# One encoder layer on one core: forward segments, maxima, unread products and the split of a matrix in other places of the program

## The chip, the cores and the metric

The kernel runs on one core of one Trainium2 chip. The engines work side by side, each through its own queue of instructions in order: TensorE (PE, with its weight loads PEld), VectorE (DVE), ScalarE (ACT), GpSimd (POOL) and SyncE (SP, which issues most DMA transfers). The metric is the device time of one execution in microseconds (us), lower is better.

## What is computed

One layer over 2048 tokens of width 1024: a normed input projected into all branches, a gated linear recurrence in both directions (4 heads, chunks of 64), dense attention (8 heads), a gated merge, a mixture of 64 experts of which each token takes two, and a gated projection of per-layer inputs. Cut to what matters here:

```python
h = rmsnorm(x, ln_mix); z = h @ w_in
# recurrence, in both directions, per head:
#   S_t = diag(f_t) S_{t-1} + k_t v_t^T ;  o_t = S_t^T q_t ; then a norm of o per head and a gate
# attention, per head and block of queries:
s = einsum('bhqd,bhkd->bhqk', q, k) * scale
o = einsum('bhqk,bhkd->bhqd', softmax(s), v)
x += w_out(sigmoid(g_A) * w_oA(A) + sigmoid(g_B) * w_oB(B))
# experts: top-1 group, top-2 in it
x += sum over two experts of weight * (silu(h @ w1[e]) * (h @ w3[e])) @ w2[e]     # h = rmsnorm(x)
x += (p @ w_ple_proj) * sigmoid(rmsnorm(x) @ w_ple_gate)
```

## The kernel before

All large products are made of three products of fp32r halves (`mm3`, lines 96 to 101): each operand is split into a high part, a copy by ACT, and a low part, a subtraction by DVE or POOL. The stages follow one another, and in each the order of every engine's instructions is the order in which the Python code emits them (`manual_schedule`). Side work is written as generators that are advanced by `next` at fixed places, so that their instructions fall between those of the main lane.

*Start* (`stage_in`, line 175). The first token tile's rows are loaded, squared, scaled and turned by eight TensorE transposes (L199) before the first product; until then TensorE has nothing to do.

*Recurrence* (`hgrn`, line 884). 16 segments (4 heads, 4 segments each, from the last token back), eight steps each. In a step the main lane does one level of `hgrn_levels`; `gates` is advanced twice, which gives nine gate products of 128x512 (L860); and `side` advances the lanes that follow a segment: `hgrn_tail`, which makes the backward outputs and saves what the forward direction needs, and, once a head's last segment is through, `hgrn_forward`, which goes over that head's four segments from the front. One forward segment is a chain that is cut by `yield`: DVE updates the state four times (h_sf, L758), PE multiplies it with the queries into h_pf (L764), DVE adds the backward outputs (L766), ACT squares (L771), DVE makes the norm (L773 to L776, ten small operations and four larger ones, h_so), PE transposes h_so into h_pf (L781), and ACT copies the result out as h_a (L784). h_pf has one buffer. `hgrn_forward` (L790) starts a segment every three of its steps, and advances all lanes in each step, the oldest first.

*Attention* (`attention`, line 964). A softmax needs the row maxima of the scores before the scores are made, so each block of 512 queries has eight `max_step`s (L1005): two 96x512 products into t_pm, which has one buffer, and a DVE reduction of them (L1015). For the first block these are made at the start, with gate products between them (`run(n)` advances `gates`, two for a chunk of nine); K and V come by SP's queue. Then the main loop makes, for each of 16 key tiles of a block (kt), the scores of a later tile (three products, t_ps), the low part of its exponentials, the products with V (two), and at every second kt one max step of the next block (`maxima`), ahead of the scores. At kt 11 alone it stands at the end of the step; the maxima of the block before it are written in that step (`rows1`).

*Merge and routing* (`merge_out`, line 1627). Per token tile: products, residual, norm, transposes (`turn`), logits, and a chain of small operations on DVE (`route`), which needs TensorE at two places (`products`, at RANKS and SLOTS). The routes of the last tile end the stage; the experts' rows are then gathered by POOL through an index table.

*Experts* (`experts`, line 1947). 64 experts, in six positions each; a product of position i uses weights that were split three positions ahead on ACT (L1984) and DVE (L1986). In nine of them (`PROJ`, every fourth from 29 on) two products of w_ple_proj with p stand beside. Its weights are loaded at expert 28 and split at the last position of the same expert (L2094, L2095).

*Last stage* (`ple`, line 2186): the rest of these projections (`project`), the experts' sums (`add`), the norm, and the gate's products.

## Time and profile before

| | |
|---|---|
| time, median of 3 runs | 3376.83 us (3375.84 to 3383.98) |
| profiled execution | 3377.6 us, of which the span of instructions 3375.8 |
| busy share | PE 96%, PEld 80%, DVE 74%, ACT 60%, POOL 35% |
| instructions | 50147 |
| mean granted clock of TensorE | 0.987 |
| DMA | 599.81 MB, mean 178 GB/s |

A profile has for each engine the time in which it is busy, and rows of single instructions with their start and duration; a bracket behind a row gives the idle time of that engine just before, and what ended it. Matmul rows overlap, since the engine is pipelined: what a product costs is the distance from its start to that of the next. The granted clock (1.00 or 0.50 in most stretches) is the share of TensorE's full 2.4 GHz that the chip gave. Products of the same shape take twice as long at half.

### The profile page before, as it was taken

To read this page: it belongs to the slowest core of one execution; us is meant where nothing else is said; L and a number is where in the kernel's file an instruction comes from. 1 tells how busy PE (TensorE), PEld (TensorE's weight loads), DVE (VectorE), ACT (ScalarE), POOL (GpSimd) and SP (SyncE) were. 2 spreads that over 40 slices of the span, in tenths; PEclk is the share of its full clock that TensorE was granted. 3 is DMA by queue.
4 is the path that set the end of the run, shared out by engine and by line. 5 is a ranking of instruction groups with operands and counts; after the bars stand their busy time and mean duration, and the time that the engine had idled before them with its cause. 6 is when DMAs were issued, how large, how long until landed. Compare 5 with 4: busy or idle time off the path is not lost. (4 is left out here: it accounts for less than half of the span.)

```text
span 3375.8 us, 50147 instructions
## 1 busy us (share of the span) xinstructions
PE 3251.5 (96%) x17616; PEld 2690.4 (80%) x17616; DVE 2490.3 (74%) x4364; ACT 2020.8 (60%) x3610; POOL 1181.8 (35%) x869
## 2 busy tenths in 40 slices
PE   7999999999989999999999999999979999999899
PEld 7898989777767787777777777878868878888687
DVE  5666555467788747888888885645679989999775
ACT  5454544457666636888888884212248888888522
POOL 0000000144445426888888883000012222222243
PEclk9999999999999999999999999999989999999999
DMA  5756574633354252111111105866469899999542
GB/s 171 246 180 210 172 230 149 240 126 107 104 184 150 82 152 78 49 46 49 46 49 27 43 17 171 239 211 227 152 238 373 323 332 354 377 364 353 200 172 112
DMA packets 340607, 599.81 MB, mean 178 GB/s; under 512 B 59168, under 2 KB 209984, under 8 KB 328063
## 3 DMA queue, kind: packets, MB, share of 16 engines
q1 hardware_dynamic: 319246, 551.55, 48.9%
q0 software_dynamic: 20688, 43.45, 3.6%
q8 instruction: 140, 2.29, 0.3%
q10 hardware_dynamic: 416, 1.57, 0.1%
q14 instruction: 117, 0.95, 0.1%
HBM read 470.47 MB, written 159.51 MB: 187 GB/s over the span
## 5 line engine op out<-in xcount | busy, mean ns | idle before, releaser
L1048 POOL TENSOR_TENSOR t_za<-t_za,t_ph 128x512 f32<-128x512 f32 x384 | 498.0, 1297 | 66.1 <-ACT t_ph L1040 45.5
L1986 DVE TENSOR_TENSOR e_wl<-e_raw,e_wh 128x1024 fp32r<-128x1024 f32 x384 | 459.4, 1220 | 48.6 <-ACT e_wh L1984 40.4
L1984 ACT ACTIVATE e_wh<-e_raw 128x1024 fp32r<-128x1024 f32 x384 | 403.0, 1069 | 26.4 <-DMA e_raw<-in_w_dram 24.0
L1015 DVE TENSOR_REDUCE t_mx<-t_pm 128x1 f32<-128x1024 f32 x256 | 313.3, 1224 | 99.4 <-PE t_pm L1014 96.5
L1040 ACT ACTIVATE t_ph<-t_ps 128x512 fp32r<-128x512 f32 x512 | 305.2, 596 | 121.7 <-PE t_ps L1038 102.3
L1053 DVE TENSOR_TENSOR t_pl<-t_ps,t_ph 128x512 fp32r<-128x512 f32 x512 | 343.0, 683 | 32.1 <-ACT t_ps L1041 27.2
L860 PE MATMUL g_pm<-g_h,g_wh 128*128 128x512 f32 x1024 | 337.5, 411 | 4.6 <-DMA g_h<-d_ht 2.7
L1041 ACT ACTIVATE t_ps<-t_ps 128x512 f32<-128x512 f32 x512 | 303.7, 593 | 0.0
L2038 POOL DMA_INDIRECT d_y<-e_raw,sly x64 | 71.8, 1121 | 469.4 <-ACT e_raw L2036 439.2
L860 PEld LDWEIGHTS g_pm<-g_h,g_wh 128*128 128x128 f32 x1024 | 184.0, 190 | 47.9 <-DMA g_h<-d_ht 3.4
L663 POOL TENSOR_TENSOR h_qq<-h_qq,h_ff 128x512 f32<-128x512 f32 x112 | 169.1, 1515 | 149.8 <-DVE h_ff L666 87.4
L99 PE MATMUL e_pg<-e_wh,e_xh 128*128 128x512 f32 x512 | 207.5, 405 | 1.6 <-ACT e_wh L1984 1.2
L100 PE MATMUL e_pg<-e_wl,e_xh 128*128 128x512 f32 x512 | 203.6, 398 | 3.4 <-DVE e_wl L1986 3.3
L1036 PE MATMUL t_ps<-t_ql,t_kh 96*128 96x512 f32 x512 | 204.9, 400 | 0.1
L101 PE MATMUL e_pg<-e_wh,e_xl 128*128 128x512 f32 x512 | 204.3, 399 | 0.6 <-DVE e_xl L1973 0.6
L1065 PE MATMUL t_pa<-t_ph,vt 128*128 128x512 f32 x512 | 203.9, 398 | 0.0
L860 PE MATMUL g_pm<-g_h,g_wl 128*128 128x512 f32 x512 | 202.8, 396 | 0.5 <-DVE g_wl L836 0.5
L1066 PE MATMUL t_pb<-t_pl,vt 128*128 128x512 f32 x512 | 202.3, 395 | 0.1
L1037 PE MATMUL t_ps<-t_qh,t_kl 96*128 96x512 f32 x512 | 202.3, 395 | 0.0
L1038 PE MATMUL t_ps<-t_qh,t_kh 97*128 97x512 f32 x512 | 202.2, 395 | 0.0
L99 PE MATMUL pm<-whi,hh 128*128 128x288 f32 x640 | 194.2, 304 | 8.1 <-ACT csb L352 4.0
L100 PE MATMUL pm<-wlo,hh 128*128 128x288 f32 x640 | 190.4, 298 | 1.0 <-DVE nx_v L215 1.0
(447 smaller groups left out, 8640.4 us busy)
## 6 DMA issues: line engine op xcount, KB each, us to landing
e_raw<-in_w_dram SPq DMA_DIRECT2D x256, 512.0 KB
e_raw<-in_w_dram SPq DMA_DIRECT2D x64, 1024.0 KB
wraw<-in_w_in_dram SPq DMA_DIRECT2D x48, 512.0 KB
wraw<-in_w_in_dram SPq DMA_DIRECT2D x40, 576.0 KB
g_wr<-in_w_in_dram SPq DMA_DIRECT2D x38, 512.0 KB
d_g<-g_o SPq DMA_DIRECT2D x64, 256.0 KB
m_g<-d_g SPq DMA_DIRECT2D x64, 256.0 KB
p_y<-d_y SPq DMA_DIRECT2D x16, 1024.0 KB
```

The costliest lines, as they stand in the source:

```text
L99: nc.tensor.matmul(out, ah, bh, start=start, stop=False)
L100: nc.tensor.matmul(out, ah, bl, start=False, stop=False)
L101: nc.tensor.matmul(out, al, bh, start=False, stop=stop)
L860: nc.tensor.matmul(pm, p, q, start=k == 0 and i == 0, stop=k == KC - 1 and i == 2)
L1015: nc.vector.tensor_reduce(mx[n, i][:, j:j + 1], pm.rearrange("p a b -> p (a b)"), axis=AX, op=OP.max)
L1036: nc.tensor.matmul(ps, kh[0:QK, ks], ql[0:QK], start=True, stop=False)
L1040: nc.scalar.activation(ph, ps, AF.Exp)
L1041: nc.scalar.activation(ps, ps, AF.Exp)
L1048: nc.gpsimd.tensor_tensor(za[n], za[n], ph.bitcast(F32), op=OP.add)
L1053: nc.vector.tensor_tensor(pl, p, ph.bitcast(F32), op=OP.subtract)
L1984: nc.scalar.activation(hi, raw, AF.Copy)
L1986: nc.vector.tensor_tensor(lo, raw, hi.bitcast(F32), op=OP.subtract)
```

## The change

Seven edits, in the order of the program. (1) At the start, POOL clears a row of hl, and 24 products of it with itself go to a buffer that nobody reads. (2) A forward segment starts every four steps; one more `yield` stands before its transposes. (3) In attention's beginning, `gates` is advanced six times before the max steps, not twenty, and twice behind each of the three `maxima` that precede the loop, not once; V's split follows the third max step. (4) In attention's loop the last two max steps of a block (kt 13 and 15) are emitted behind the scores. (5) In the merge's tail unread products of the identity stand at four places, and 20 before expert 0's transposes. (6) `PROJ` starts at expert 30; the load of w_ple_proj stays at expert 28, and its split goes to the end of expert 29. (7) In the last stage the parts of the next projection are made before the first `yield` of `project`, and `add(1)` stands ahead of the loop.

```diff
@@ -317,6 +317,11 @@
         gB = const.tile([128, D], F32, name="gB")
         nc.scalar.dma_start(gB, bcast_rows(ln_mix[0], D))
         hh, hl, xt, v = open_norm(0, 1)
+
+        nc.gpsimd.memset(hl[:, 0].bitcast(F32), 0.0)
+        pm = psum.tile([128, 512], F32, name="pm", bufs=2)
+        for _ in range(24):
+            nc.tensor.matmul(pm, hl[:, 0, 0:128], hl[:, 0], start=True, stop=True)
         raws = load_raw(*todo[0][1:3])
         xt += [load_x(i) for i in range(1, 4)]
         squares(hh, xt[0], v, 0)
@@ -776,6 +781,7 @@
             nc.vector.scalar_tensor_tensor(so[:, c], op[:, c], r[:, c:c + 1], so[:, c], op0=OP.mult, op1=OP.mult)
         yield
         yield
+        yield
         pt = psum.tile(SH, F32, name="h_pf", bufs=1)
         for c in range(HC):
             nc.tensor.transpose(pt[:, c], so[:, c], g.ident)
@@ -787,7 +793,7 @@
     lanes = []
     for seg in range(NTB):
         lanes.append(segment(seg))
-        for _ in range(3):
+        for _ in range(4):
             for lane in lanes:
                 next(lane, None)
             yield
@@ -1144,11 +1150,11 @@
         for tb in range(NTB):
             load_k(h, tb)
         vr = load_v(h)
-        for _ in range(NTB):
-            run(5)
-        split_v(h, vr)
+        run(6)
         for s in range(8):
             max_step(0, s)
+            if s == 2:
+                split_v(h, vr)
             if s == 4 and NB > 1:
                 load_q(1)
             run(2)
@@ -1157,7 +1163,7 @@
         rows1(0)
         for u in range(-MAX_LEAD, 0):
             maxima(u)
-            run(1)
+            run(2)
         late.work, late.psum = more()
         for u in range(LEAD):
             scores(u)
@@ -1186,10 +1192,12 @@
             if kt == 14:
                 sums1(n)
 
-            if kt != 16 - MAX_LEAD:
+            if kt < 16 - MAX_LEAD:
                 maxima(u)
             if u + LEAD < NB * NK:
                 scores(u + LEAD)
+            if kt > 16 - MAX_LEAD:
+                maxima(u)
             if u + LEAD - 1 < NB * NK:
                 low(u + LEAD - 1)
             if kt == 1:
@@ -1734,6 +1742,12 @@
             step(r)
             if r.state is not END:
                 return
+
+    def idle(n):
+
+        py = psum.tile([128, 512], F32, name="m_py", bufs=OUT_BANKS["m_py"])
+        for _ in range(n):
+            nc.tensor.matmul(py[:, 0:128], g.ident, g.ident, start=True, stop=True)
 
     def advance(n, weave=()):
 
@@ -1777,12 +1791,16 @@
     advance(0, norm(NU - 1))
     after(PRE_B)
     products()
+    idle(8)
     turn(NU - 1)
     turned(NU - 1)
+    idle(2)
     logits(NU - 1)
     advance(100)
+    idle(6)
     products()
     logged(NU - 1)
+    idle(14)
     while routes:
         for r in list(routes):
             if r.state not in (RANKS, SLOTS):
@@ -1917,7 +1935,7 @@
 PRE, PRE_A, PRE_B = 8, 4, 2
 PRES = ((2, 48), (2, 60), (2, 72), (2, 84))
 MORE_LAST = 48
-PROJ = range(29, 29 + 4 * 9, 4)
+PROJ = range(30, 30 + 4 * 9, 4)
 
 
 def stage_moe(tc, g, w1, w3, w2, p, w_proj, ln_ple, out):
@@ -2042,6 +2060,10 @@
     proj, units = None, iter(range(T // 128))
     for i in range(3):
         split(i)
+
+    pt = psum.tile([128, 4, 128], F32, name="e_pt")
+    for _ in range(20):
+        nc.tensor.matmul(pt[:, 0], g.ident, g.ident, start=True, stop=True)
     for h in range(2):
         turn(0, h)
         turned(0, h)
@@ -2049,7 +2071,7 @@
         with_proj = e in PROJ
         if e and e + NX - 1 < NE:
             moe_gather(nc, g, xgs[(e - 1) % NX], g.ti[0:n, e + NX - 1:e + NX])
-        if e == PROJ[0] - 1:
+        if e == PROJ[0] - 2:
             g.prees.close()
             ppool = g.es.enter_context(tc.tile_pool(name="pproj", bufs=1, side="right", reuse_waits="tile"))
             g.pp = [ppool.tile([128, D], F32, name=f"pp{t}") for t in range(T // 128)]
@@ -2287,15 +2309,15 @@
     def project(u):
 
         nonlocal q
-        py = proj.product(q, 0)
+        parts = q
+        py = proj.product(parts, 0)
         if u + 1 < NU:
             proj.turn()
             proj.load(nc.sync if u < u0 + 1 else nc.gpsimd)
+            q = proj.parts(others[(u + 1 - u0) % 2])
         yield
         proj.out(u, 0, py, True)
-        py = proj.product(q, 1)
-        if u + 1 < NU:
-            q = proj.parts(others[(u + 1 - u0) % 2])
+        py = proj.product(parts, 1)
         yield
         proj.out(u, 1, py, True)
 
@@ -2326,6 +2348,7 @@
             weave(rows)
         if u == u0 + FIRST + 1:
             weave(norm(0))
+            weave(add(1))
     m.x = g.ef.tile([128, 2, D], F32, name="e_raw")
     m.h = g.ef.tile([128, 2, KC, 128], F32R, name="e_raw")
     load_x(2)
@@ -2337,8 +2360,6 @@
             nc.sync.dma_start(out[0, (u - 1) * 128:u * 128], st[u - 1].x)
         load_x(u + 3)
         pg = product(u, 0)
-        if u == 0:
-            weave(add(1))
         weave(norm(u + 1), add(u + 2) if u else ())
         finish(u, 0, pg, nc.vector if last else nc.gpsimd)
         if last:
```

How the order moves, at three places. First ACT in the recurrence, around the first copy h_a of a head (h_op and h_qf are saved by `hgrn_tail`; h_j, h_ss are the squares of the next forward segment). Before:

```order
L729 ACTIVATE h_op<-h_po 128x512
L731 ACTIVATE h_qf<-h_qq 128x512
L784 ACTIVATE h_a<-h_pf,gon 128x512
L656 ACTIVATE h_ku<-h_kk 128x512
L664 ACTIVATE h_qq<-h_qq 128x4x2x64
L877 ACTIVATE g_o<-g_pm 128x512
L688 ACTIVATE h_at<-h_ab 64x4x64 x2
L688 ACTIVATE h_at<-h_ps 64x4x64 x2
L771 ACTIVATE h_j,h_ss<-h_op 128x128 x4
```

After (lines are five to six further down):

```order
L734 ACTIVATE h_op<-h_po 128x512
L736 ACTIVATE h_qf<-h_qq 128x512
L776 ACTIVATE h_j,h_ss<-h_op 128x128 x4
L661 ACTIVATE h_ku<-h_kk 128x512
L669 ACTIVATE h_qq<-h_qq 128x4x2x64
L790 ACTIVATE h_a<-h_pf,gon 128x512
L883 ACTIVATE g_o<-g_pm 128x512
```

The copy h_a stood ahead of the following segment's squares; it now stands behind them.

Second, PE in attention's loop, from kt 11 to kt 13 (t_pm maxima, t_ps scores, t_pa and t_pb products with V). Before:

```order
L1014 MATMUL t_pm<-t_kh,t_qh 128x512 x2
L1036 MATMUL t_ps<-t_ql,t_kh 128x512
L1037 MATMUL t_ps<-t_qh,t_kl 128x512
L1038 MATMUL t_ps<-t_qh,t_kh 128x512
L1065 MATMUL t_pa<-t_ph,vt_13243 128x512
L1066 MATMUL t_pb<-t_pl,vt_13243 128x512
L1014 MATMUL t_pm<-t_kh,t_qh 128x512 x2
```

After:

```order
L1020 MATMUL t_pm<-t_kh,t_qh 128x512 x2
L1042 MATMUL t_ps<-t_ql,t_kh 128x512
L1043 MATMUL t_ps<-t_qh,t_kl 128x512
L1044 MATMUL t_ps<-t_qh,t_kh 128x512
L1071 MATMUL t_pa<-t_ph,vt_13315 128x512
L1072 MATMUL t_pb<-t_pl,vt_13315 128x512
L1042 MATMUL t_ps<-t_ql,t_kh 128x512
L1043 MATMUL t_ps<-t_qh,t_kl 128x512
L1044 MATMUL t_ps<-t_qh,t_kh 128x512
L1020 MATMUL t_pm<-t_kh,t_qh 128x512 x2
```

Five products stood between the two pairs of maxima; now there are eight.

Third, PE in the merge's tail, from the last tile's transposes to the end of the stage (m_py is the unread buffer, r_pc the ranks). Before:

```order
L1694 MATMUL m_pt<-ident,mn_h 128x128 x8
L1707 MATMUL m_pl<-wr,m_ht 128x72 x8
L1331 LDWEIGHTS tri
L1331 MATMUL r_pc<-r_ohb,tri 128x64
L1334 LDWEIGHTS ones
L1334 MATMUL r_pc<-ohs,ones 128x64
```

After:

```order
L1750 MATMUL m_py<-ident 128x128 x8
L1702 MATMUL m_pt<-ident,mn_h 128x128 x8
L1750 MATMUL m_py<-ident 128x128 x2
L1715 MATMUL m_pl<-wr,m_ht 128x72 x8
L1750 MATMUL m_py<-ident 128x128 x6
L1339 LDWEIGHTS tri
L1339 MATMUL r_pc<-r_ohb,tri 128x64
L1342 LDWEIGHTS ones
L1342 MATMUL r_pc<-ohs,ones 128x64
L1750 MATMUL m_py<-ident 128x128 x14
```

Unread products now stand ahead of each of these steps of the queue.

## Rows read from the trace of the kernel before

**Rows 1.** Stretches: us; PE, PEld, DVE, ACT, POOL busy; clock; DMA share; GB/s.
```profile
700.00:1160.00 460.00, 430.08 (x3621) 343.23 (x3620) 371.01 (x643) 301.30 (x587) 228.57 (x132) 0.99 0.41 124
2830.00:3130.00 300.00, 297.94 (x1437) 246.06 (x1436) 272.21 (x313) 246.29 (x355) 70.05 (x56) 1.00 0.99 364
22.00:24.00 2.00, 1.34 (x4) 0.99 (x5) 1.86 (x8) 1.56 (x3) 0.00 (x0) 0.50 0.00 0
```

**Rows 2.** Waits of PE in the recurrence, 690 to 1235 us: total, times, longest.
```profile
PE h_pf L764 <- ACT h_a L784: 11.3, 6, 2.6
PE h_pt L693 <- DVE h_kk L661: 6.4, 5, 2.5
...
PE h_pf L781 <- issue: 4.0, 5, 2.8
```

**Rows 3.** Timeline of DVE, one forward segment: start, us, engine, line, instruction.
```profile
1204.64 0.16 DVE L72 SCALAR_TENSOR_TENSOR h_r_y<-h_r_a,h_r_y 128x4 f32<-128x4 f32 x1
1204.84 1.14 DVE L776 SCALAR_TENSOR_TENSOR h_so<-h_op,h_r_y,h_so 128x128 f32<-128x128 f32 x4
...
1206.50 1.51 DVE L758 SCALAR_TENSOR_TENSOR h_sf<-h_sf,h_fe,h_kv 128x128 f32<-128x128 f32 x4
```

**Rows 4.** Timeline of PE at attention's first and last uncovered maxima.
```profile
1257.11 0.64 PE L1014 MATMUL t_pm<-t_kh,t_qh 96*128 96x512 f32 x2
...
1278.17 1.22 PE L1014 MATMUL t_pm<-t_kh,t_qh 96*128 96x512 f32 x2 [1.32 <-DVE t_mx L1015]
```

**Rows 5.** Timeline of SP: the first K load.
```profile
1238.01 0.43 SPq L985 DMA_DIRECT2D t_kh<-d_kh  x1
```

**Rows 6.** Waits of PE in attention's loop, 1300 to 2040 us.
```profile
PE t_pm L1014 <- DVE t_mx L1015: 4.7, 30, 0.2
```

**Rows 7.** Timeline of PE in one block of attention's loop.
```profile
1326.70 0.39 PE L1036 MATMUL t_ps<-t_ql,t_kh 96*128 96x512 f32 x1
...
1327.62 0.39 PE L1066 MATMUL t_pb<-t_pl,vt 128*128 128x512 f32 x1
1328.17 0.73 PE L1014 MATMUL t_pm<-t_kh,t_qh 96*128 96x512 f32 x2 [0.16 <-DVE t_mx L1015]
1328.74 0.39 PE L1036 MATMUL t_ps<-t_ql,t_kh 96*128 96x512 f32 x1
```

**Rows 8.** Timeline of PE at the start.
```profile
11.02 1.97 PE L199 MATMUL pt<-ident,xt 128*128 128x128 f32 x8 [11.02 <-DVE xt L219]
...
20.66 1.10 PE L199 MATMUL pt<-ident,xt 128*128 128x128 f32 x8 [1.79 <-DVE xt L219]
```

**Rows 9.** Timeline of PE in the merge's tail and expert 0.
```profile
2470.01 3.69 PE L1707 MATMUL m_pl<-wr,m_ht 128*128 128x72 f32 x16
...
2487.81 1.95 PE L1965 MATMUL e_pt<-ident,xg 128*128 128x128 f32 x8 [5.69 <-ACT e_wh L1984]
...
2492.53 0.63 PE L99 MATMUL e_pg<-e_wh,e_xh 128*128 128x512 f32 x1
2492.96 0.63 PE L100 MATMUL e_pg<-e_wl,e_xh 128*128 128x512 f32 x1
```

**Rows 10.** Timeline of POOL there.
```profile
2473.81 2.74 POOL L1932 MEMSET xg<- 128x1024 f32 x3 [242.31 <-PE r_pc L1334]
```

**Rows 11.** Timeline of DVE there.
```profile
2474.52 2.07 DVE L1345 TENSOR_SCALAR r_rk<-j,rr 128x128 bf16<-128x128 bf16 x1
```

**Rows 12.** Timeline of ACT at the split of w_ple_proj.
```profile
2771.81 1.06 ACT L2094 ACTIVATE e_raw<-pp 128x1024 fp32r<-128x1024 f32 x1 [3.20 <-DMA pp<-in_w_ple_proj_dram]
```

**Rows 13.** Timeline of PE there: the ends of the stretch.
```profile
2771.18 0.40 PE L101 MATMUL e_pg<-e_wh,e_xl 128*128 128x512 f32 x1
...
2784.58 0.40 PE L99 MATMUL e_pg<-e_wh,e_xh 128*128 128x512 f32 x1
```

**Rows 14.** Waits of ACT for the weights, 2830 to 3130 us.
```profile
ACT e_wh L1984 <- DMA e_raw<-in_w_dram: 23.6, 26, 1.5
```

**Rows 15.** Timeline of PE in the last stage.
```profile
3162.65 0.79 PE L101 MATMUL p_pp<-e_raw,p_ql 128*128 128x512 f32 x1 [2.70 <-DVE p_ql L1898]
```

## The prediction

> **What bounds the kernel now.** I read four views: the busy time by stretches, to see in which stages TensorE has holes; the waits of TensorE in those stages, for who ends the holes; the timelines around them, for what one hole costs; and the granted clock beside it, because a hole can also make the work behind it run at half speed. In every stage TensorE is the engine that sets the time: in the recurrence with the gates it is busy 430.08 of 460 us at a clock of 0.99, in the experts 297.94 of 300 us [rows 1]. So a gain can only come from a hole of TensorE that closes, or from work at half clock that comes to run at full clock; and extra work on any other engine costs only what lands on TensorE. Where TensorE has almost no hole, as in the experts, the DMA engines stand at a share of 0.99 [rows 1]: there a second bound lies right behind the first.
>
> **Forward segments, four steps apart.** The scores of the next segment (L764) and the transposes of this one (L781) share the one buffer h_pf. TensorE waits at L764 for ACT's copy h_a 6 times, 11.3 us in all, and at L781 5 times, 4.0 us; on top, 6.4 us at L693 for DVE's h_kk [rows 2]. That is 21.7 of the 29.9 us of holes (460 less 430.08) of this stretch. A fourth step gives h_a one more step of gate products before the buffer is asked for, so the first two items, 15.3 us, go where DVE doesn't bring them back. DVE is the risk: a segment's norm is a chain of small operations about 0.2 us apart that ends with h_so (1.14 us), and the state update is another 1.51 us [rows 3]. With three steps these fell into different steps; with four, the norm of one segment and the update of the next stand in the same one. On the other side a segment's DVE work is now spread over four steps, which is what helps the 6.4 us. I take 12 us: 15.3 less a fifth for what the stacking gives back; bounds 3 (only some waits go) and 20 (all three items). That each head's forward part now lasts 21 side steps and not 17 costs nothing while other heads run; after the last head it takes four more sides with gate products between, which are work that has to be done anyway, and comes out of the next part.
>
> **Attention's beginning.** After the last transposes TensorE now runs twelve gate chunks of nine products before the first maxima at 1257.11; the last maxima then stand without cover, each waiting 1.32 us for DVE, and run at half speed (1.22 us for a pair that takes 0.64) [rows 4]. The change leaves chunks for these places. Four such waits are 5.3 us and the pairs and products at half speed some 1 to 3 more. Against it: the first K load is issued at 1238.01 [rows 5], 19 us ahead of its first use; with seven chunks fewer before it, at 2.1 us each by the pitch below, that shrinks to about 4 us, for a load whose neighbours are queued on the same SP. I take 4 us; bounds 1 and 6.
>
> **Attention's loop.** The pair of maxima at position 11 of a block's 16 stands last in its step, the next, at 13, first: only five products stand between them on the single t_pm buffer, and DVE's reduction isn't over in that time. The profile lists 30 waits and 4.7 us [rows 6], but the timeline shows that the hole is larger than what is listed: products stand 0.23 us apart (four steps from 1326.70 to 1327.62), while from 1327.62 to 1328.74, three products, it takes 1.12 us instead of 0.70 [rows 7]. The excess is 0.42 us, and a hole of this kind stands in 30 blocks: 12.6 us. The change puts the scores' three products in between: 8 × 0.23 = 1.84 us, where the buffer came free 1.47 us after the pair before (1326.70 to 1328.17). So the hole closes with 0.4 us to spare; DVE's own order is the same, so its t_pl isn't moved past a reduction. The next pair, at position 1, now has eight products and not eleven in front: same sum, it holds. I take 12.5; bounds 4.7 (only the listed part) and 13.
>
> **Start.** The first eight transposes take 1.97 us, the same eight at 20.66 take 1.10: the engine starts at half speed, although nothing before it ran [rows 8]. 24 unread products in the idle 11 us before them, behind a POOL memset, can be over by then: at half speed, 0.43 us each [rows 9], 10.3 us at most. Full speed from the first transposes gives back 0.87 us there, and little behind, because DVE and ACT pace the first rows (the transposes at 20.66 waited 1.79 us for DVE). I take 1; bounds 0 and 3. From 22 to 24 us the clock stands at 0.50 [rows 1], right behind a stretch in which transposes were all that TensorE did. The Trainium skill, "TensorE: Matmul & The Clock Gate", "Part 4: PE-mode transpose", says that transposes don't count as busy for the clock in the way that products do; by that rule it would fall again between the unread products and the first real ones, and this term would be 0.
>
> **Tail of the merge, and expert 0.** The last token tile runs at half speed: logits take 3.69 us, the experts' first transposes 1.95, and the products behind them stand 0.43 us apart and not 0.23 until 2496 [rows 9]. TensorE sat idle 5.69 us before these transposes. The unread products cost twice: those ahead of a real instruction delay it when they run longer than the hole (by the logits' row, 16 passes in 3.69 us, about 0.46 us for one of two passes at half clock, half of that at full), and gain by the clock. The 20 before expert 0 thus last 4.6 to 9.2 us against a hole of 5.69: from 1.1 early to 3.5 late. What they can win is 0.9 us of transposes and 0.2 on each of 13 products, 3.5 together. A second gain: POOL's memset of xg, which waits for the rows' last product, runs 2.74 us from 2473.81 [rows 10]; in that time DVE's r_rk at 2474.52 takes 2.07 us [rows 11], a write of 128x128 bf16. With turn and logits at full clock, 2.7 us shorter, and the unread eight mostly in the hole, the memset ends about as r_rk starts: up to 2.07 back, I take 1.7. The six before the ranks delay those by what the faster logits won. Together I take 1.5; bounds −3 (all 20 at half speed in front of expert 0, nothing else won) and +4.
>
> **w_ple_proj.** The split of this matrix waits on ACT 3.20 us for the load that the same expert issued [rows 12], with the experts' own splits queued behind it; TensorE needs 13.4 us from 2771.18 to 2784.58 [rows 13], for 19 products of 0.23 and six transposes, about 5 us, so 8 lost. One expert later the load has long landed; what stays is two copies of 1.06 us on ACT and two subtractions on DVE ahead of an expert's own splits, 1.6 us. That makes 6.6. But the weights' transfers go on while TensorE waits, and ACT's splits wait for them 26 times, 23.6 us, from 2830 on [rows 14]: part of what is won here is lost there. I take 5; bounds 1 and 8. The Trainium skill, "DMA: Bandwidth & Descriptors", "Where 436 GB/s comes from", puts the limit of a core's HBM traffic at about 358 GB/s; the stretch with share 0.99 shows 364 [rows 1]. By that rule the transfers bound that stretch, and the whole 5 would be given back.
>
> **The last stage.** The parts of the next projection are made before the yield, not behind it, and add(1) moves ahead of the loop. The 2.70 us hole at 3162.65 [rows 15] stays, since p_ql there stands behind add(0) on DVE, which waits for a load; one shorter such hole goes, and add(1)'s two large operations now stand before the first row's split. I take 0.5; bounds −2 and +2, by less than the one row.
>
> **The sum.** 12 + 4 + 12.5 + 1 + 1.5 + 5 + 0.5 = 36.5. The profiled execution took 3377.6 us (span 3375.8); it lies 0.8 us above the median of 3376.83. 3377.6 − 36.5 = 3341.1, so **3341 us**.
>
> **Rivals.** Times are again from 3377.6.
> - *DVE has room:* the fourth step closes all three items of the recurrence (20 rather than 12), and the split's delay is hidden (8 rather than 5): 3341 − 11 = 3330. For it: DVE is busy 371 of 460 us. Against: its work comes in bursts.
> - *The stacked step keeps the waits:* norm and update in one step shift the waits to h_sf and h_so, 3 us won instead of 12, and the beginning of attention waits for its K load (1 instead of 4): 3341 + 12 = 3353.
> - *The transfers bound the experts:* the 5 us of the split come back as waits of e_wh: 3346. For it: the share of 0.99; against: TensorE is busy 99% there as well. The limit named under w_ple_proj says the same.
> - *Unread products hold no clock:* between them and the first real products stand only transposes, and the clock falls as at 22 us [rows 1]. Start 0, and the 20 products run at 0.46 in front of expert 0: 1.5 becomes −3. 3341 + 5.5 = 3347, rounded up. The rule on transposes named under the start says the same.
> - *Slower than before:* one mechanism, in the recurrence. If TensorE's in-order queue stands still at L764 for as long as the stacked DVE step lasts, some 2.1 us of small operations, 1.14 and 1.51 [rows 3], 4.7 together, in each of 16 segments, that is 75 us of holes instead of 21.7: 53 lost, 24.5 won elsewhere, 3406. It decides from 46 us of holes on (2.9 per segment), where it eats all the rest. Against it: every step also holds nine gate products, 2.1 us, that TensorE may run meanwhile where they stand ahead of L764.
>
> **Chances.** Forecast 0.46, DVE has room 0.16, stacked step 0.15, transfers 0.11, no clock 0.07, slower 0.05. A measurement tells about 0.3%, 10 us, from no change; faster means below 3367. All of the forecast's own range lies there, 3330 to 3352 (the terms' bounds, taken as independent), and of the rivals all but the last; of the stacked step a third may come near the limit. So faster 0.90, same 0.06, slower 0.04. The range 3325 to 3360 leaves out the slower rival, the tail of the stacked step, and the case that all bounds come out at their best.
>
> **What the profile would show.** Right: no or few waits of h_pf on h_a between 700 and 1160, and TensorE over 440 us busy there; no waits of t_pm on t_mx in the loop, and blocks 0.4 us shorter; a half clock no more at 2470 to 2496; no hole over 2 us at the split. Wrong: new waits of h_pf on h_sf or h_so's transposes of a step's length; the K load ending the first waits of attention; more and longer waits of e_wh on the weights after the split; a clock of 0.50 behind the unread products.

## The result, and the profile after

The changed kernel takes 3404.81 us (median of 4 runs, 3399.70 to 3406.13) against 3377.27 us before (4 runs): a ratio of 1.0075, 95% interval 1.0057 to 1.0092. It is slower by 27.5 us; forecast was a gain of 36. The profiled execution has a span of 3404.3 us, TensorE busy for 3280.1 us of it (96%), at a mean clock of 0.985 (0.987 before).

Where the time went is read from the first and last starts of single source lines. Each line below gives the number of instructions, their shortest, median and longest duration in ns, and the start of the first and of the last in us. The lines are the recurrence's first products h_ps, the scores, the products with V, the transposes of the experts' rows and of the last stage's. In the kernel before:

```profile
L650 PE MATMUL h_ps<-h_q,h_ku x256: 222/222/371, 678.4 to 1150.3; 128*64 128x64 f32 x128
...
L1036 PE MATMUL t_ps<-t_ql,t_kh x512: 389/393/628, 1281.7 to 2047.2; 96*128 96x512 f32 x171
...
L1066 PE MATMUL t_pb<-t_pl,vt x512: 387/396/505, 1287.4 to 2050.1; 128*128 128x512 f32 x171
...
L1965 PE MATMUL e_pt<-ident,xg x512: 270/273/453, 2487.8 to 3127.6; 128*128 128x128 f32 x171
...
L2243 PE MATMUL e_pt<-ident,pn_h x128: 271/272/444, 3169.4 to 3356.0; 128*128 128x128 f32 x128
```

The same lines of the changed kernel:

```profile
L655 PE MATMUL h_ps<-h_q,h_ku x256: 222/222/369, 675.5 to 1170.7; 128*64 128x64 f32 x128
...
L1042 PE MATMUL t_ps<-t_ql,t_kh x512: 389/394/628, 1299.4 to 2069.0; 96*128 96x512 f32 x171
...
L1072 PE MATMUL t_pb<-t_pl,vt x512: 387/396/505, 1306.0 to 2071.9; 128*128 128x512 f32 x171
...
L1983 PE MATMUL e_pt<-ident,xg x512: 270/273/378, 2514.5 to 3150.4; 128*128 128x128 f32 x171
...
L2265 PE MATMUL e_pt<-ident,pn_h x128: 272/273/302, 3194.9 to 3384.5; 128*128 128x128 f32 x128
```

The differences of these starts give a length for each stage (the last turn of the merge, 2469.7 and 2490.2, is read the same way from L1694 and L1702):

| stage | before | changed | difference |
|---|---|---|---|
| to the first h_ps product | 678.4 | 675.5 | −2.9 |
| recurrence and attention's beginning, to the first scores | 603.3 | 623.9 | +20.6 |
| attention's loop | 768.4 | 772.5 | +4.1 |
| merge, to the last turn | 419.6 | 418.3 | −1.3 |
| tail, to expert 0's first transposes | 18.1 | 24.3 | +6.2 |
| experts, to their last transposes | 639.8 | 635.9 | −3.9 |
| to the last transposes of the last stage | 228.4 | 234.1 | +5.7 |

The experts' −3.9 is expert 0 alone, whose products the unread ones have brought to full clock: from its second transposes on it is 629.8 and 630.1. Each length comes from one profiled execution. Among the profiles of the runs below that have the same code in a stage, the first row lies between 673.6 and 677.2, the second between 621.6 and 624.5, the loop between 771.6 and 772.7, the experts' between 631.9 and 635.9, and the last stage's between 232.8 and 236.6, so a difference of 3 us in one row of one profile says little, except in the loop. The border between the last two rows moves too: with `PROJ` one expert later, six products of w_ple_proj, 1.4 us, fall behind the experts' last transposes and not ahead of them, so that 1.4 of the +5.7 are work that has only changed its row.

**Recurrence.** TensorE's waits there (columns as in [rows 2]), and the same stretch as in [rows 1], of the changed kernel:

```profile
PE h_pf L769 <- DVE h_sf L763: 38.3, 12, 6.4
```

```profile
700.00:1160.00 460.00, 419.50 (x3432) 337.16 (x3432) 335.67 (x608) 289.83 (x557) 216.22 (x126) 0.95 0.39 120
2848.00:3148.00 300.00, 296.54 (x1423) 242.83 (x1422) 269.55 (x309) 244.84 (x354) 68.54 (x56) 1.00 0.98 363
```

The waits for h_a are gone, as meant, and 38.3 us of waits for h_sf have come, the longest 6.4. TensorE is busy for 419.50 us where it was 430.08, and the clock has fallen from 0.99 to 0.95, which makes the work between the waits dearer. One of them, on DVE and on PE:

```profile
848.68 0.15 DVE L778 TENSOR_SCALAR h_ss<-h_ss 128x4 f32<-128x4 f32 x1
...
852.11 1.12 DVE L763 SCALAR_TENSOR_TENSOR h_sf<-h_sf,h_fe,h_kv 128x128 f32<-128x128 f32 x3
```

```profile
850.15 0.39 PE L769 MATMUL h_pf<-h_sf,h_qf 128*128 128x128 f32 x2
852.51 1.26 PE L769 MATMUL h_pf<-h_sf,h_qf 128*128 128x128 f32 x6 [1.97 <-DVE h_sf L763]
```

PE asks at 850.15 for states that DVE makes at 852.11, behind the whole norm of the segment before (848.68 to 852.1). The step has both, and the older lane's norm comes first on DVE (its h_so starts at 851.05).

**Attention's loop.** The waits of t_pm on t_mx [rows 6] are gone, and 30 others stand in their place:

```profile
PE t_ps L1042 <- DVE t_pl L1059: 7.3, 30, 0.2
```

```profile
1347.23 0.62 PE L1020 MATMUL t_pm<-t_kh,t_qh 96*128 96x512 f32 x2
...
1349.32 0.40 PE L1074 MATMUL t_pb<-t_ph,zo 128*128 128x512 f32 x1
1349.96 0.50 PE L1042 MATMUL t_ps<-t_ql,t_kh 96*128 96x512 f32 x1 [0.24 <-DVE t_pl L1059]
```

```profile
1347.89 1.23 DVE L1021 TENSOR_REDUCE t_mx<-t_pm 128x1 f32<-128x1024 f32 x1 [0.50 <-PE t_pm L1020]
...
1349.22 1.28 DVE L1059 TENSOR_TENSOR t_pl<-t_ps,t_ph 128x512 fp32r<-128x512 f32 x2
```

The line of waits gives 0.2 us for each, but the hole is again larger than what is listed. The maxima of kt 13 now start at 1347.23, behind the scores, so their reduction ends at 1349.1; only then comes t_pl, which frees one of the three t_ps buffers, and the scores of the next step wait for it: 0.64 us from 1349.32 to 1349.96 where 0.23 is the pace.

**Tail and expert 0.** PE and ACT around the 20 unread products (L2066):

```profile
2507.20 7.46 PE L2066 MATMUL e_pt<-ident 128*128 128x128 f32 x40 [6.10 <-DVEq L2143]
2514.50 1.06 PE L1983 MATMUL e_pt<-ident,xg 128*128 128x128 f32 x8
2515.79 0.50 PE L99 MATMUL e_pg<-e_wh,e_xh 128*128 128x512 f32 x1 [0.23 <-ACT e_xh L1989]
...
2520.29 0.49 PE L1983 MATMUL e_pt<-ident,xg 128*128 128x128 f32 x3
```

```profile
2507.12 1.28 ACT L2002 ACT_TABLE_LOAD   x1 [11.84 <-DVEq L2143]
...
2515.14 1.09 ACT L1989 ACTIVATE e_xh<-e_pt 128x512 fp32r<-128x512 f32 x2 [3.77 <-PE e_pt L1983]
```

The 6.10 us hole is the branch behind the routing: TensorE and ACT stand at it until the flag that DVE writes has been read, and the unread products stand behind it, not in it. They then take 7.3 us. Part of that time is ACT's, which loads its table and splits the first weights until 2511.4; the rest delays the transposes. The logits did come to full clock (2.00 us, not 3.69 [rows 9]), and DVE's r_rk, which ends with POOL's memset as before, takes 1.3 us less of the 2.07 [rows 11], where 1.7 was forecast:

```profile
2494.91 0.77 DVE L1353 TENSOR_SCALAR r_rk<-j,rr 128x128 bf16<-128x128 bf16 x1
```

So the flag is written 17.2 us after the last tile's ptab products instead of 18.6. The way from the flag (noi) to ACT's first instruction behind the branch, its table load, then took longer: 4.55 us, where the kernel before needs 1.79. Before:

```profile
2483.60 0.15 DVE L1384 CAST noi<-r_no 128x1 int32<-128x1 f32 x1
```

```profile
2485.39 1.28 ACT L1984 ACT_TABLE_LOAD   x1 [10.50 <-ACTq L2121]
```

And changed:

```profile
2502.57 0.15 DVE L1392 CAST noi<-r_no 128x1 int32<-128x1 f32 x1
```

From the last tile's ptab products to expert 0's second transposes it is 34.9 us and was 32.8. Of these +2.1, the flag makes −1.4, the branch +2.8, and what stands behind the branch +0.7 (13.2 us from the table load to the second transposes, against 12.5).

**w_ple_proj and the last stage.** ACT at the place where weights follow the load of w_ple_proj, and PE in the last stage:

```profile
2802.35 1.06 ACT L2002 ACTIVATE e_wh<-e_raw 128x1024 fp32r<-128x1024 f32 x1 [5.78 <-DMA e_raw<-in_w_dram]
...
2805.00 2.00 ACT L2116 ACTIVATE e_raw<-pp 128x1024 fp32r<-128x1024 f32 x2
```

```profile
3170.83 0.50 PE L99 MATMUL p_pp<-e_raw,p_qh 128*128 128x512 f32 x1 [0.50 <-ACT pp L1929]
...
3187.86 0.50 PE L101 MATMUL p_pp<-e_raw,p_ql 128*128 128x512 f32 x1 [1.95 <-DVE p_ql L1916]
...
3199.43 0.79 PE L99 MATMUL e_pg<-wG_h,p_hh 128*128 128x512 f32 x1 [3.51 <-ACT p_hh L2276]
```

The split itself (2805.00) waits for nothing now; but before it ACT stands for 5.78 us waiting for an expert's weights. In the last stage there are four waits of 0.5 us as at 3170.83, and 3.51 us before the first gate product.

**Start.** This part came as forecast:

```profile
1.61 8.55 PE L324 MATMUL pm<-hl 128*128 128x512 f32 x24 [1.61 <-POOL hl L321]
10.96 1.09 PE L199 MATMUL pt<-ident,xt 128*128 128x128 f32 x8 [0.79 <-DVE xt L219]
...
13.40 0.29 PE L99 MATMUL pm<-whi,hh 128*128 128x288 f32 x1
13.53 0.29 PE L100 MATMUL pm<-wlo,hh 128*128 128x288 f32 x1
```

The 24 products end before 10.2 us, the eight transposes take 1.09 instead of 1.97 [rows 8], and the products behind them stand 0.13 us apart.

### The profile page after: what moved, and what is told of

It is laid out like the page before. It is cut to its first block, busy times and chain, and to the rows that moved or that the text cites. A ratio compares the mean times of both kernels' runs of the same rounds, so it can differ in the third digit from the quotient of the medians.

```text
span 3404.3 us, 50453 instructions
## 1 busy us (share of the span) xinstructions
PE 3280.1 (96%) x17740; PEld 2717.3 (80%) x17740; DVE 2458.5 (72%) x4364; ACT 2018.7 (59%) x3610; POOL 1179.7 (35%) x870
```

## The experiments

Each was made from the changed kernel by the edit shown. Stage lengths are measured as in the table above.

### Newest lane first, and one more yield

```diff
-            for lane in lanes:
+            for lane in reversed(lanes):
```

> The changed kernel with one word more: in hgrn_forward the lanes are advanced newest first, so that on DVE the state update of segment k+1 stands ahead of the norm of segment k in the step that they share. Theory (order: TensorE's 38.3 us of waits for h_sf are the time that the update stands behind the norm's chain): those waits fall under 8 us, no wait of that size comes up for h_so, and the stretch from the first h_ps product to the first scores, 603.3 us before and 623.9 in the changed kernel, comes to 585 to 600; the whole to about 3377 to 3383. Rival (amount: a step with both has more DVE work than a step lasts, whatever its order): the waits move to h_so or h_op, and the stretch stays above 615, the whole above 3394.

Measured: 3373.09 us, 4 us below the expected 3377 to 3383, a ratio to before of 0.999 (0.998 to 1.000); the stretch takes 592.5 us, 31.4 less than in the changed kernel. The waits are down to 12.2 us:

```profile
PE h_pf L769 <- DVE h_sf L763: 12.2, 8, 2.9
```

"Under 8" was missed as well: eight waits for the update are left, though it now stands ahead of the norm. The second edit leaves the lanes in their old order and puts an empty step between the update and its product:

```diff
         state.sf = sf
         yield
+        yield
         po = psum.tile(SH, F32, name="h_pf", bufs=1)
```

> The changed kernel with one more yield in a forward segment, between the state update and the product with the queries; segments four steps apart, oldest lane first as in the changed kernel. Norm and update still share their step, on DVE in the order of the changed kernel, but TensorE asks for the update one step later. Theory (order and place: what cost 20.6 us is that TensorE's queue reaches the product in the step in which the update is made): the 38.3 us of waits for h_sf fall under 4 us, and the stretch from the first h_ps product to the first scores comes to 586 to 593 us (592.5 with the newest lane first, 603.3 before, 623.9 changed). Rival (amount of DVE's work in the shared step): the level's own products h_ps and h_pt, which stand behind it on DVE, take the waits over, and the stretch stays above 600.

Measured: 590.1 us, one execution 3369.03 in all. No wait for h_sf is left in the list:

```profile
PE h_ps L679 <- ACT h_ku L661: 11.8, 14, 1.9
PE h_pf L788 <- issue: 10.7, 6, 2.6
```

The stretch is 33.8 us shorter with the same instructions. But the edit does two things at once, and what was expected of it says only one. The product comes two steps behind its update, not one. And the norm, which follows the product, comes a step later too, so that the next segment's update no longer shares a step with it and stands ahead of it on DVE:

```profile
828.60 1.51 DVE L763 SCALAR_TENSOR_TENSOR h_sf<-h_sf,h_fe,h_kv 128x128 f32<-128x128 f32 x4
...
834.32 1.14 DVE L782 SCALAR_TENSOR_TENSOR h_so<-h_op,h_r_y,h_so 128x128 f32<-128x128 f32 x4
```

So this run alone does not show what the distance is worth while both share a step. The first edit decides the question: it keeps the same work in the shared step, turns only its order round, and gets 31.4 us back. It is the order on DVE that cost them, not the amount of its work; the 2.4 us between the two edits are within what profiles of the same code differ by. Other waits are left. The transposes have 10.7 us where they had 4.0 [rows 2], and h_ps 11.8 where it had 6.3 in the kernel before:

```profile
PE h_ps L674 <- ACT h_ku L656: 6.3, 10, 1.9
```

With them, four steps so mended are worth about 7 us against three (590.1 against 597.5 in the next run), not the forecast's 12.

### Three steps again

```diff
-        for _ in range(4):
+        for _ in range(3):
...
-        yield
         pt = psum.tile(SH, F32, name="h_pf", bufs=1)
```

> The changed kernel with the recurrence as before: segments three steps apart, one yield fewer. Theory (the fourth step alone is the loss in this stretch, and the new beginning of attention gains 3 to 5 us): the stretch from the first h_ps product to the first scores comes to 598 to 601 us (603.3 before, 623.9 changed), the whole to 3379 to 3382. Rival (the beginning of attention loses too, for its K loads come late): the stretch stays at 606 or more, the whole at 3387 or more.

Measured: 3378.39 us, ratio 1.0005 (0.9996 to 1.0015), and 597.5 us for the stretch. The fourth step alone costs 26.4 us here, and the rest of this stretch, attention's new beginning, gains 5.8, as the theory has it; both numbers lie half a us below the expected ranges.

### Maxima in the loop

```diff
-            if kt > 16 - MAX_LEAD:
-                maxima(u)
             if u + LEAD - 1 < NB * NK:
                 low(u + LEAD - 1)
+            if kt > 16 - MAX_LEAD:
+                maxima(u)
```

> The changed kernel with the subtraction t_pl emitted ahead of the late maxima at kt 13 and 15, not behind them. Theory (the loop's new wait of t_ps on t_pl is the subtraction that stands on DVE behind a reduction which now starts 0.7 us later): the 30 waits of t_ps on t_pl go, those of t_pm on t_mx stay away, and the loop from the first scores to the last product with V takes 755 to 760 us (768.4 before, 772.5 changed). Rival (DVE has no room there for both in any order): the 30 waits go to another tile, and the loop stays above 766.

Measured: the loop takes 762.3 us. The 30 waits for t_pl are gone, but seven at kt 1 are listed:

```profile
PE t_pm L1020 <- DVE t_mx L1021: 2.7, 7, 0.4
```

That is half right: the subtraction was what the 30 waits stood for, but the waits of t_pm did not stay away, and the loop is 2.3 us over the expected range. The pair at kt 15, now late on DVE as well, isn't read when that at kt 1 is due. So only kt 13 was moved:

```diff
-            if kt < 16 - MAX_LEAD:
+            if kt not in (16 - MAX_LEAD, 18 - MAX_LEAD):
                 maxima(u)
...
-            if kt > 16 - MAX_LEAD:
-                maxima(u)
             if u + LEAD - 1 < NB * NK:
                 low(u + LEAD - 1)
+            if kt == 18 - MAX_LEAD:
+                maxima(u)
```

> The changed kernel's loop with only the maxima at kt 13 behind the scores and behind t_pl, and those at kt 15 ahead of the scores as before. With both moved and t_pl ahead, 7 waits of t_pm at kt 1 remained and the loop took 762.3 us. Theory (the pair at kt 15, moved late, is what makes the pair at kt 1 wait): no waits of t_pm or t_ps remain, and the loop takes 755 to 759 us. Rival (DVE is too full there for any order): waits at kt 15 or 1 remain, and it stays above 761.

Measured: 757.1 us, 11.3 less than before, and 709.71 of 710 us busy:

```profile
1340.00:2050.00 710.00, 709.71 (x3107) 576.26 (x3106) 623.53 (x871) 594.40 (x1092) 605.48 (x462) 1.00 0.15 41
```

The list of waits has no t_pm and no t_ps any more. Nearly all of the forecast's 12.5 us was there to be had, by another order.

### Unread products

```diff
-    pt = psum.tile([128, 4, 128], F32, name="e_pt")
-    for _ in range(20):
-        nc.tensor.matmul(pt[:, 0], g.ident, g.ident, start=True, stop=True)
```

> The changed kernel without the 20 unread products ahead of expert 0's transposes. Theory (TensorE can't start them before the branch behind the routing, so they delay expert 0 by their own 7.3 us and give back 4.2 by the clock): from the last tile's ptab products behind its norm to expert 0's second transposes 31 to 32.5 us (34.9 in the changed kernel, 32.8 before), the first transposes at half speed again (1.9 us for eight). Rival (without them the clock stays low much longer): over 34.5 us.

Measured: 33.7 us, 1.2 better than the changed kernel and 0.9 worse than before, between the theory's range and the rival's. The transposes run at half speed again, and what comes behind the branch is not TensorE's alone:

```profile
2505.80 1.94 PE L1983 MATMUL e_pt<-ident,xg 128*128 128x128 f32 x8 [6.25 <-DVEq L2140]
2510.39 0.79 PE L99 MATMUL e_pg<-e_wh,e_xh 128*128 128x512 f32 x1 [2.65 <-ACT e_xh L1989]
...
2517.31 0.60 PE L1983 MATMUL e_pt<-ident,xg 128*128 128x128 f32 x4
```

```profile
2505.61 1.28 ACT L2002 ACT_TABLE_LOAD   x1 [11.88 <-DVEq L2140]
```

The first product waits 2.65 us for ACT, whose three splits and table load begin at the branch too; so 7.3 us of unread products cost only 4, and the clock gives back 2.4 of them. Whether the 20 cost anything hangs on the branch. In us, with the rows read as for the changed kernel:

| kernel | from the flag to ACT's table load | from there to the second transposes |
|---|---|---|
| before, no products there | 1.8 | 12.5 |
| the mended ones below, no products there | 1.8 | 13.0 and 13.1 |
| one more yield, the 20 there | 1.8 | 12.9 |
| this run, no products there | 4.6 | 11.7 |
| changed, the 20 there | 4.6 | 13.2 |

Behind a quick branch the 20 cost nothing that shows, behind a slow one 1.5 us. In the kernels without them and with a quick branch the transposes stand 4.4 us behind POOL's gather of the experts' rows, and in the second mended one the profile names these rows as what they wait for.

Next the 20 were put ahead of the branch (taken out where they stood), and the 24 at the start left out; the added lines:

```diff
...
     nc.vector.tensor_copy(g.noi, no)
+    py = psum.tile([128, 512], F32, name="m_py", bufs=OUT_BANKS["m_py"])
+    for _ in range(20):
+        nc.tensor.matmul(py[:, 0:128], g.ident, g.ident, start=True, stop=True)
```

> The changed kernel with the 20 unread products of the experts moved ahead of the branch behind the routing, and without the 24 at the start. Theory (ahead of the branch TensorE has a hole of 6.1 us that nobody needs, so they cost nothing there and keep the clock): the first transposes of expert 0 take 1.1 us and not 1.9, and from the last tile's ptab products behind its norm to expert 0's second transposes it takes 31 to 32 us (34.9 changed, 33.7 without them, 32.8 before). At the start the transposes of the third and fourth rows' tile come 0.7 to 0.8 us later again (28.12 us in the changed kernel, 28.85 before). Rival (the clock falls again in the wait for ACT's first splits, 2.65 us): over 33 us.

Measured: 33.7 us, as without them: the rival's number. The transposes are at full speed, but TensorE then waits for ACT:

```profile
2504.63 7.32 PE L1391 MATMUL m_py<-ident 128*128 128x128 f32 x40
2512.57 1.13 PE L1982 MATMUL e_pt<-ident,xg 128*128 128x128 f32 x8 [0.61 <-PEq L2139]
2515.76 0.50 PE L99 MATMUL e_pg<-e_wh,e_xh 128*128 128x512 f32 x1 [2.07 <-ACT e_xh L1988]
```

The rival's mechanism shows as well: behind that wait the products stand 0.43 us apart from 2518.1 to 2520.2, at a granted clock of 0.69 to 0.81. And the 20 take longer (7.32 us) than the hole, so that TensorE gets past the branch 1.6 us later than ACT. At the start, the transposes of the third and fourth tiles' rows come at 28.80 us, 0.68 later than in the changed kernel: the 24 products there are worth 0.7 us.

How long the branch takes differs between profiles: ACT's table load, its first instruction behind it, begins 1.8 us after the flag in five of them (before, three steps, one more yield, and both mended kernels) and 4.5 to 4.9 us after it in nine, the changed kernel among them. Every kernel has one profile, so whether an edit sets this or chance does isn't shown; the cause stays open. It is why the tail's row varies by some 3 us, and it hides what the 20 are worth.

### The load of w_ple_proj

```diff
-                nc.sync.dma_start(g.pp[14 + k], w_proj[0, k * 128:(k + 1) * 128, :])
+                nc.gpsimd.memset(g.pp[14 + k], 0.0)
```

> The changed kernel with w_ple_proj's two tiles cleared by POOL instead of loaded (1 MB less by DMA; the projection's results are then zero); its split and all else stay. Theory (the experts are bound by the weights' transfers from there on, so the place of the split moves nothing, and the load itself is the cost): ACT's 5.8 us wait for the weights at the split goes, and the experts, from the first to the last transposes of rows, take 630 to 633 us (635.9 changed). Rival (the split's copies and subtractions are the cost): TensorE's waits for e_wh and e_wl there stay, and the stretch is 635 or more.

Measured: 630.4 us, below the eight profiles that have the load and the same start (631.9 to 635.9), and TensorE's wait of 3.0 us for e_wh at this place is gone; of ACT's 5.8 us, 2.3 are left. It speaks for the transfers, though the margin over the scatter is 1.5 us. What decides is how long a gain at this place lasts, which the mended kernels below show.

### The last stage

Two kernels, each with one of its two edits undone:

```diff
-        parts = q
-        py = proj.product(parts, 0)
+        py = proj.product(q, 0)
...
-            q = proj.parts(others[(u + 1 - u0) % 2])
         yield
         proj.out(u, 0, py, True)
-        py = proj.product(parts, 1)
+        py = proj.product(q, 1)
+        if u + 1 < NU:
+            q = proj.parts(others[(u + 1 - u0) % 2])
```

```diff
-            weave(add(1))
...
         pg = product(u, 0)
+        if u == 0:
+            weave(add(1))
```

> The changed kernel with project as before (the next projection's parts behind its yield); add(1) stays ahead of the loop. Theory (both edits of the last stage lose: the parts ahead of the yield put ACT's copy p_qh ahead of the copy that frees p_pp, four waits of 0.5 us, and add(1) delays the first rows): those four waits go, a wait of p_ql of 2 to 3 us comes back, and the stretch from the last transposes of the experts' rows to those of the last stage's takes 232 to 235 us (234.1 changed, 228.4 before). Rival (project alone is the loss): 228 to 230.

> The changed kernel with add(1) behind the first product again; project stays changed. Theory (add(1) ahead of the loop is most of the loss in the last stage: ACT's square and DVE's sums wait there for a load and stand ahead of the first rows' halves): TensorE's 3.5 us wait for p_hh falls under 1 us, and the same stretch takes 228 to 231 us. Rival (project is the loss): 233 or more.

Measured: 234.1 us with project undone, 231.6 with add(1) undone, 234.1 changed and 228.4 before. The kernel to compare with is not the one before, whose `PROJ` puts 1.4 us of products into another row, but the first of the mended ones below: 229.7 with the last stage as before and `PROJ` from 30 on. With project undone the four waits of 0.5 us go, that of p_ql is 1.83 us and not the expected 2 to 3, and the one for p_hh grows:

```profile
3192.99 0.80 PE L99 MATMUL e_pg<-wG_h,p_hh 128*128 128x512 f32 x1 [4.43 <-ACT p_hh L2276]
```

With add(1) undone that one is 0.31 us, and the four stay. So add(1) ahead of the loop loses some 3 us by its wait for p_hh, though the 231.6 lie half a us over the expected range and only 1.2 under the scatter of the changed code. Of project it is shown that its four waits, 2.0 us, come with the edit; that the stage loses by them is argued, since 234.1 is the changed kernel's own number and TensorE, without them, waits as much longer for p_hh.

### Mended

```diff
         state.sf = sf
         yield
+        yield
...
+            if kt == 18 - MAX_LEAD:
+                maxima(u)
...
-    for _ in range(20):
-        nc.tensor.matmul(pt[:, 0], g.ident, g.ident, start=True, stop=True)
```

(the maxima as in the second edit of the loop; the last stage wholly as before)

> The changed kernel mended by what the runs showed: a yield between the state update and its product, maxima behind scores and behind t_pl at kt 13 alone, no unread products ahead of expert 0, and the last stage as before. Theory (the stages add up): against the kernel before, the recurrence with attention's beginning 590 us (603.3), the loop 757 (768.4), the start 0.7 less, the merge's tail 1 less, the last stage 228 to 230 (228.4), the split of w_ple_proj 0: 25 us less in all, a ratio of 0.991 to 0.994. Rival (what one stage wins, the next gives back, as the transfers of weights or the branch): less than 15 us, a ratio over 0.9955.

> The same with PROJ as before, so the split of w_ple_proj at the expert that issued its load. Theory (the weights' transfers bound the experts there, so the split's place is worth nothing): within 3 us of the kernel that runs beside it, though TensorE has the hole of 13 us around the split again. Rival (the forecast's price): 5 to 7 us slower.

Measured, beside the kernel before at 3375.65 us: 3344.56 us for the first, a ratio of 0.9902 (0.9885 to 0.9918), and 3344.17 us for the second, 0.9899 (0.9882 to 0.9917). The stages of the first: 587.0 for the recurrence with attention's beginning, 756.0 for the loop, 229.7 for the last stage; 31 us less in all, 6 more than the sum expected, and so a ratio a little better than the expected 0.991 to 0.994. The two differ by 0.4 us in the median, but four runs of each spread over 7 and 8 us, and that alone doesn't rule out the forecast's 5. The traces settle it. Time from the first transposes of expert 10's rows to those of later experts:

| to expert | 30 | 34 | 44 | 60 |
|---|---|---|---|---|
| before (split at the expert of the load) | 195.6 | 238.0 | 300.4 | 508.6 |
| changed (one expert later) | 188.7 | 236.3 | 299.0 | 508.5 |
| first mended (one expert later) | 188.7 | 235.8 | 299.5 | 508.0 |
| second mended (at the expert of the load) | 195.2 | 236.6 | 299.0 | 509.7 |

The later split puts TensorE 6.5 to 6.9 us ahead at expert 30, and by expert 44 no more than 1.4 are left, in the mended pair nothing. Waits of ACT around the split, with the split one expert later, and at the expert of the load (where e_wh waits 0.5 us besides):

```profile
ACT e_wh L2003 <- DMA e_raw<-in_w_dram: 9.5, 6, 5.1
```

```profile
ACT e_raw L2114 <- DMA pp<-in_w_ple_proj_dram: 3.9, 2, 2.8
```

The wait changes its name, from the load of w_ple_proj to that of the weights which stand behind it in the queue, and grows.

## Why the prediction was wrong

- **Recurrence** (forecast −12, measured +26.4 for the fourth step alone). This is the step that failed: "I take 12 us: 15.3 less a fifth for what the stacking gives back". The stacking gave back all of the 15.3 and 26.4 more: in 12 places TensorE stands for the state update, which DVE makes behind the norm of the segment before, 38.3 us in all, and the clock falls from 0.99 to 0.95. The mechanism had been seen, and named as the slow rival, with 4.7 us for each of 16 segments. It was 3.2 us on average, so the argument against it, the nine gate products that TensorE may run meanwhile, held in part; and 12 waits, since the first segment of each of the four heads has no norm ahead of it. The error was to take the stacked step for a small loss, and to give the rival 1 chance in 20. The order decides most of it: with it turned round, 31.4 us came back. That the whole came to 3404.8, beside the rival's 3406, is partly luck: its recurrence lost half of its 53 us, and the 24.5 us that it counted as won elsewhere weren't won. Of the 64 us between forecast and measurement, 38 lie here.
- **Attention's loop** (−12.5, measured +4.1), the second step that failed, with 17 of the 64 us. "DVE's own order is the same, so its t_pl isn't moved past a reduction": the order is the same, but the reduction starts 0.7 us later, and all that is behind it on DVE moves with it. I had checked who waits for the moved instruction, and not who waits for the one behind it. The size of the hole was right: 11.3 us came back when t_pl went first and only kt 13 was moved.
- **Attention's beginning** (−4, measured −5.8): inside its bounds, by single profiles that scatter by 3 us. The K loads stopped nothing; TensorE has two waits of 1.3 us left there.
- **Start** (−1, measured −0.7): right. It may be somewhat more, since the two profiles without the 24 have 678.4 and 679.0 in the table's first row, and the twelve with them 673.6 to 677.2. The rule that transposes don't count for the clock (the Trainium skill, "TensorE: Matmul & The Clock Gate", "Part 4: PE-mode transpose") would have made it 0; here the transposes and the products behind them ran at full speed, so no run shows it at this place. From 22 to 24 us the clock still stood at 0.50, as before.
- **Tail** (−1.5, measured +2.1 up to expert 0's second transposes). The flag comes 1.4 us sooner, by the logits and r_rk, much as forecast. The step that failed is the hole of 5.69 us: only its last 2.4 us, from ACT's table load on, lie behind the branch, and the 20 products, which can't pass it, don't fit in there. The rest of the loss is the slow branch, whose cause is open.
- **w_ple_proj** (−5, measured 0). The rival of the transfers was right: the lead that the later split gives is gone some ten experts on, and ACT's wait changes its name, from the load of w_ple_proj to the weights behind it in the queue. From 2848 to 3148 us the transfers moved 363 GB/s at a share of 0.98. The Trainium skill, "DMA: Bandwidth & Descriptors", "Where 436 GB/s comes from", puts a core's HBM limit at about 358 GB/s; this mean lies within 2% of it, but a slice of 85 us on the changed kernel's page has 376, so no run shows 358 as a ceiling.
- **Last stage** (−0.5, measured +5.7, of which 1.4 only changed its row). I named the order of ACT for neither edit: parts stand ahead of the copy that frees p_pp, and add(1)'s square ahead of the first rows' halves.

The rival of unread products that hold no clock was wrong as well: they do raise it, at the price of their own time where they aren't in a hole.

## What to carry to other kernels

When an instruction is moved later on one engine, follow what it releases one step further: on the engine that consumes it, everything queued behind the consumer moves too, and one of those may free a buffer that the first engine needs next. In lanes that share a step, ask which lane's instructions come first on the engine that makes what the bounding engine needs next: turning the order round was worth 31 us here, with not one instruction more, and an empty step that took the norm out of the update's step 34. And where the weights' transfers already run nearly all the time (a share of 0.98 here), a hole of TensorE may be nothing to be won back: closing this one put it 6.5 us ahead at expert 30, and by expert 44 the lead was gone.

## What was not expected of the hardware

From the flag to ACT's first instruction behind the branch it took 1.8 us in five profiles and 4.5 to 4.9 in nine, with the same code there; no run shows why.

The 20 products of 128x128 f32 behind the branch took 7.3 us from a granted clock of 0.50, between the 9.2 and 4.6 us that the prediction worked out for the two levels. The clock rose while they ran, unread as they are: 0.50 from 2507 to 2511 us, 0.72 up to 2514.5, and 1.00 behind.

The granted clock's record isn't the pace of each product. In the kernel before it reads 1.00 from 10 to 15 us, though the eight transposes there take 1.97 us [rows 8], against 1.09 in the changed kernel, and the products behind them stand 0.24 us apart, not 0.13. What a clock is worth is read from the rows.
